# Triangular inverses of an RWKV-7 block: operands fetched two steps ahead, results written over them, a second buffer for the decays

## Chip, cores and metric

One core of one Trainium2 chip runs the whole kernel. The metric is device time in microseconds (us), the median of three runs.

## What is computed

Two layers of a block on 1280 tokens (256 of context, 1024 latent), 1024 wide. Each layer normalises, projects, mixes tokens in three ways (retention, gated linear attention, RWKV-7), projects back and runs a gated FFN. The part that matters here is RWKV-7's recurrence with six heads of 64, which the reference runs token by token, in both directions:

```python
def step(s, inp):
    rt, wt, kt, vt, kkt, at = inp
    sa = jnp.einsum("bhvk,bhk->bhv", s, -kkt)
    s = s * wt[:, :, None, :] + sa[..., None] * (kkt * at)[:, :, None, :] + vt[..., None] * kt[:, :, None, :]
    return s, jnp.einsum("bhvk,bhk->bhv", s, rt)
```

The kernel does it in chunks of 64 tokens. Within a chunk the rank-one corrections form a triangular system, so each chunk and head needs a 64x64 strictly triangular matrix (products of kk and kk*a, weighted by the decays between two tokens) and the inverse of one plus it.

## The kernel before

Operands lie with 128 channels on partitions (two heads a column block, three blocks). `rwkv_in` (L459) makes, by layer, the columns of RWKV's input projection; `col` (L487) is one column block: 72 or so dense products on TensorE, copied out by ScalarE, convolved by VectorE. Each finished row of operands (decay sums, kk, kk*a, k, r) goes to DRAM with `rw_row` (L648), in a tensor named `ops` that is indexed by 64-token chunk. Once decay sums, kk and kk*a are there, `rwkv_in` starts the generator `rw_inverses` (L681) and takes three or four of its steps between two columns of the rest of the projection (L600 to L606), and what is left at the end (L632). After that the next stage starts with the dense products of `gla_in` and the scan `rwkv` (L1233), which reads the inverses.

One step u of twenty (a forward and a backward chunk each) does this:

- X, a slot of tag `a` (AB = 5 slots), gets the chunk's operands from `ops` by two DMAs, one a direction (`rw_load`, L655 to L669, all issued by SyncE through L248). In traces this is `a<-ops`; the text calls the pair *fetch u*.
- ScalarE takes the exponential of the decay sums into P (one buffer, L671) and into X itself (L672), by L238.
- VectorE forms M in T, a second slot of tag `a`, by L679 and L694.
- TensorE multiplies (L701, through L245: `pn<-a`), VectorE masks the result into A, the last third of T (L702 through L640).
- A goes to DRAM (L703: `af<-a`); the text calls it *store u*.

After every fourth step `rw_inverse` (L708) reads four stored steps back (`L<-af`, four DMAs) and inverts their 32x32 diagonal blocks on GpSimd, some 60 instructions one after another (L718 to L728), then writes them out (`xe<-L`, `xe<-LT`, three DMAs each). There are five such recursions a layer.

The program is recorded in Python order, and a scheduler then orders each engine's instructions by priority and by when it expects operands and slots. Each engine, and SyncE's queue of DMAs, runs its list strictly in order. A DMA that has to wait for a semaphore therefore holds all DMAs behind it. Names in the queue beside the above: `wraw` weights, `gb` and `vt` finished results, `c<-ops` a row read back, `X<-ops`, `SAV`, `XE` the scan's operands.

```python
X = self.t(p, [128, PW], "a", bufs=AB)[:, 0:1152].rearrange(...)
ops = self.rw_load(l, P, X, u)
T = self.t(p, [128, PW], "a", bufs=AB)
```

Of the kernel before, what the change touches and what calls it, by code (L numbers as in the profile page):

```python
# [49 lines left out]
C2 = 1  # L50
PA = 7
NR = 2
AB = 5
HP = 5000,4500,4500
N1, N2 = 2,20
NS = 4
# [3 lines left out]
PW = TOK + 1  # L60
# [10 lines left out]
def rw_where(u):  # L71

    ns = [(0, 1), (1, 0)][u // 2] if u < 4 else (u // 2, 11 - u // 2)
    return [(ns[0], u % 2), (ns[1], 1 - u % 2)]
# [96 lines left out]
class Kern:  # L171
# [200 lines left out]

    def split_norm(self, x, b, A, B, s, xh, xl, pe=False):

        nc = self.nc
        n = BLK[b][1]
        rs = self.rstd(x, b, pe)
        for kt in range(KT):
            v = self.tmp()[:, :n]
            nc.vector.tensor_tensor(v, x[:, kt, :], rs, op=ALU.mult)  # L380
            self.act(v, v, AF.Identity, bias=B[:, kt, s:s + 1], scale=A[:, kt, s:s + 1])
            nc.scalar.copy(xh[:, kt, :], v)  # L382
            nc.vector.tensor_tensor(xl[:, kt, :], v, xh[:, kt, :].bitcast(F32), op=ALU.subtract)  # L383

    def norm_here(self, x, b, A, B, s):

        n = BLK[b][1]
        rs = self.rstd(x, b)
        for kt in range(KT):
            v = self.tmp()[:, :n]  # L390
            self.nc.vector.tensor_tensor(v, x[:, kt, :], rs, op=ALU.mult)
            self.act(x[:, kt, :], v, AF.Identity, bias=B[:, kt, s:s + 1], scale=A[:, kt, s:s + 1])

# [15 lines left out]
    def xn_tiles(self, blocks):  # L409
        xh, xl = {}, {}  # L410
        for b in blocks:
            A = self.A2 if b == 2 else self.A01
            xh[b] = self.t(A, [128, KT, BLK[b][1]], f"xh{b}", F32R)
            xl[b] = self.t(A, [128, KT, BLK[b][1]], f"xl{b}", F32R)
# [44 lines left out]
    def rwkv_in(self, l, V, W1, xh, xl, ctx_out):  # L459
# [56 lines left out]
        def zeros():  # L516
            if l:
                return
            zero = self.t(p, [128, PW], "a", bufs=AB)[:, 0:96]
            nc.gpsimd.memset(zero, 0.0)  # L520
# [44 lines left out]
        for j in range(3):  # L565
            a = self.t(p, [128, PW], "a", bufs=AB)
            for o, n in NB:
# [71 lines left out]
    def rw_masked(self, o, ps, m):  # L639
        self.nc.vector.tensor_tensor(o, ps, m.unsqueeze(1).to_broadcast([m.shape[0], 3, 64]), op=ALU.mult)  # L640

    def rw_P(self, p):
        P = self.t(p, [128, 2, 3, 66], "P")
        self.nc.gpsimd.memset(P[:, 0, :, 0:1], 1.0)
        self.nc.gpsimd.memset(P[:, 1, :, 65:66], 1.0)
        return P

# [4 lines left out]
            x = t[:, o:o + 64 * (c1 - c0)].rearrange("p (c x) -> p c x", x=64)  # L652
            self.dma(*((x, m) if back else (m, x)))

    def rw_load(self, l, P, X, u):  # L655


        half = float(np.exp(-0.5))
        lo = 15 - X.shape[2]
        src = self.OPS[l]  # L660
        r = []
        for d, (n, c) in enumerate(rw_where(u)):
            w = 2 * n + c
            if d == 0:
                self.dma(X[:, d], src[:, w, lo:15])
            else:
                if lo < 6:
                    self.dma(X[:, d, 0:6 - lo], src[:, w, lo:6])
                self.dma(X[:, d, 6 - lo:15 - lo], src[:, w, 9:18])  # L669
            cu, kk, kka = (X[:, d, o - lo:o - lo + 3] for o in ((12, 6, 9) if d else (6, 9, 12)))  # L670
            self.act(P[:, d, :, 1:65], cu, AF.Exp, scale=-half)  # L671
            self.act(cu, cu, AF.Exp, scale=half)  # L672
            r.append((cu, kk, kka))
        return r

    def rw_decayed(self, dst, ops, P):

        for d in range(2):
            self.nc.vector.tensor_tensor(dst[:, d, :, 0:64], ops[d][1], P[:, d, :, 2 * d:2 * d + 64], op=ALU.mult)  # L679

    def rw_inverses(self, l, p):  # L681

        nc = self.nc
        P = self.rw_P(p)
        for u in range(20):
            bi, w = u // 4, slice(6 * (u % 4), 6 * (u % 4) + 6)
            X = self.t(p, [128, PW], "a", bufs=AB)[:, 0:1152].rearrange("p (d i x) -> p d i x", d=2, x=64)
            ops = self.rw_load(l, P, X, u)
            T = self.t(p, [128, PW], "a", bufs=AB)
            M = T[:, 0:768].rearrange("p (d j x) -> p d j x", d=2, j=3)  # L690
            A = T[:, 768:1152].rearrange("p (h x) -> p h x", h=6)
            self.rw_decayed(M, ops, P)
            for d in range(2):
                nc.vector.tensor_tensor(M[:, d, :, 64:128], ops[d][2], ops[d][0], op=ALU.mult)  # L694
            for e in range(2):
                R = slice(64 * e, 64 * e + 64)
                ps = self.pn()
                for j in range(3):
                    for d in range(2):
                        a, k = M[R, d, j, 0:64], M[R, d, j, 64:128]  # L700
                        self.mm(ps[64 * d:64 * d + 64, 64 * j:64 * j + 64], *((a, k) if d else (k, a)))  # L701
                self.rw_masked(self.rw_heads(A, e), ps[:, 0:192].rearrange("p (j x) -> p j x", j=3), self.rwmask[:, 0:64])  # L702
            self.dma(self.AF[l][bi][:, w], A)  # L703
            if u % 4 == 3:
                self.rw_inverse(l, bi)
            yield
# [526 lines left out]
    def rwkv(self, l, V, ctx_out):  # L1233
# [7 lines left out]
        P = self.rw_P(p)  # L1241
# [5 lines left out]
        def pre(u):  # L1247
            out = ctx_out or u >= 4
            lo = 0 if out else 3
            X = self.t(p, [128, 2, 15, 64], "X", bufs=XB)[:, :, lo:15]  # L1250
            ops = self.rw_load(l, P, X, u)
            AR = self.t(p, [128, 2, 3, 128], "AR", bufs=NB)
            BK = self.t(p, [128, 2, 3, 128], "BK", bufs=2)
            PC = self.t(p, [128, 2, 3], "PC", bufs=NB)
# [63 lines left out]
        def step(u, B):  # L1318
            old = S[0]
            AR, SA, SR, BKT, SAV, PC, XE = (B[x] for x in ("AR", "SA", "SR", "BKT", "SAV", "PC", "XE"))  # L1320
            T = [slice(64 * d, 64 * d + 64) for d in D]
            O = [slice(64 - 64 * d, 128 - 64 * d) for d in D]
            pa = self.pr("a", 1)
            for h in range(6):
                for d in D:
                    self.mm(pa[T[d], 64 * h:64 * h + 64], SA[O[d], h, :], SAV[O[d], d, 64 * h:64 * h + 64],
                            start=h == 0, stop=old is None and h == 5)
            if old is not None:
                for j in range(3):
                    for d in D:  # L1330
                        self.mm(pa[T[d], 128 * j:128 * j + 128], AR[:, d, j, 0:64], old[:, d, j, :], start=False, stop=j == 2)
            R0 = self.t(p, [128, 384], "R0")
            nc.scalar.copy(R0, pa[:, 0:384])
            ps = self.pr("s", 1)
            for h in range(6):
                for d in D:
                    self.mm(ps[T[d], 64 * h:64 * h + 64], XE[T[d], h, 0:64], R0[T[d], 64 * h:64 * h + 64])
            nc.scalar.copy(SAV[T[0], 0, :], ps[T[0], 0:384])
# [41 lines left out]
        with hp(1):  # L1380
            cur = [pre(u) for u in range(2)]
        yield
        for u in range(20):
            with hp(0):
                step(u, cur[u])
            if u + 2 < 20:
                with hp(1):
                    cur.append(pre(u + 2))
            yield
# [587 lines left out]
```

## Time and profile before

| | |
|---|---|
| median of 3 runs | 4083.36 us (4080.87 to 4087.71) |
| profiled execution, its own time | 4084.64 us |
| its span, first to last instruction | 4082.9 us |
| TensorE busy | 3765.2 us, 92% |
| VectorE busy | 2572.8 us, 63% |
| ScalarE busy | 1779.2 us, 44% |
| GpSimd busy | 1570.2 us, 38% |
| DMA engines busy, own queue of SyncE | 47.1% |
| mean granted TensorE clock | 0.961 |

The span is a little shorter than the time, by what lies before the first and behind the last instruction. A busy TensorE is not one at its peak, since its instructions overlap; its idle time is what the views of waits explain. In rows of a timeline the column behind the start is the length; SyncE's rows show how long issuing took, not how long the transfer ran. "<-" after an idle time names what ended it.

### The profile page before, as it was taken

The numbers are of one execution on the slowest core, as the hardware profiler recorded it, in microseconds if no ns is written. First come the engines' busy times: TensorE is split into PE (matmuls) and PEld (weight loads), VectorE is DVE, ScalarE is ACT, GpSimd is POOL, SyncE is SP. The second block draws the span as 40 slices with busy tenths as digits, with TensorE's granted clock in tenths as the row PEclk, the third lists the DMA queues.
The fourth block names the chain that finished last, engine by engine and source line by source line (L and its number), as shares of the span: only waits on it lengthen the run. The fifth ranks groups of instructions, "written<-read, shape, count | busy, mean of one in ns | idle before, by whom it ended". The sixth has DMA issues, their size and how long they took to land. (4 is left out here: it accounts for less than half of the span.)

```text
span 4082.9 us, 78226 instructions
## 1 busy us (share of the span) xinstructions
PE 3765.2 (92%) x30344; PEld 3128.7 (77%) x30344; DVE 2572.8 (63%) x4522; ACT 1779.2 (44%) x3578; POOL 1570.2 (38%) x1714
## 2 busy tenths in 40 slices
PE   7998999889998999999979997999898988999998
PEld 4776888776687988888758676887766768999886
DVE  3565757667746766665862565667658578556666
ACT  5443334234436744443545443334234465434442
POOL 1155640333435823224436145740424443223443
PEclk9998999999999999999989998999989989999999
DMA  7487545566516522225424387555654232222542
GB/s 226 107 239 186 139 125 154 172 186 193 172 60 220 186 75 85 81 83 211 158 105 141 94 233 200 136 140 147 202 183 150 88 141 101 74 84 96 182 164 101
DMA packets 626355, 594.09 MB, mean 146 GB/s; under 512 B 315452, under 2 KB 517440, under 8 KB 607680
## 3 DMA queue, kind: packets, MB, share of 16 engines
q1 hardware_dynamic: 625696, 588.04, 47.1%
q8 instruction: 240, 3.93, 0.4%
q0 software_dynamic: 288, 1.05, 0.1%
q14 instruction: 131, 1.07, 0.1%
HBM read 442.67 MB, written 146.28 MB: 144 GB/s over the span
## 5 line engine op out<-in xcount | busy, mean ns | idle before, releaser
L1456 POOL TENSOR_TENSOR slo<-raw,shi 128x512 fp32r<-128x512 f32 x511 | 730.6, 1446 | 1082.1 <-ACT shi L1455 1004.8
L1455 ACT CAST shi<-raw 128x512 fp32r<-128x512 f32 x522 | 319.5, 621 | 520.3 <-PE pd L245 207.3
L439 POOL TENSOR_TENSOR wlo<-wraw,whi 128x512 fp32r<-128x512 f32 x120 | 168.8, 1415 | 413.1 <-ACT whi L438 407.3
L245 PE MATMUL pd<-wlo,xh 128*128 128x256 f32 x1072 | 315.1, 294 | 1.3 <-POOL wlo L439 1.3
L1746 DVE TENSOR_TENSOR f<-pm,f 128x512 f32<-128x512 f32 x320 | 219.5, 688 | 153.3 <-PE pm L245 152.1
L245 PE MATMUL pd<-whi,xh 128*128 128x256 f32 x1072 | 314.7, 295 | 0.5 <-DVE st L443 0.5
L245 PE MATMUL pd<-whi,xl 128*128 128x256 f32 x1072 | 313.7, 293 | 0.0
L245 PE MATMUL pm<-hh,shi 128*128 128x512 f32 x704 | 277.2, 395 | 9.8 <-ACT hh L1726 5.4
L245 PE MATMUL pd<-xh,whi 128*128 128x512 f32 (+1 forms) x720 | 273.2, 380 | 10.0 <-ACT xh L382 8.2
L245 PE MATMUL pm<-hl,shi 128*128 128x512 f32 x704 | 275.8, 392 | 0.3 <-DVE hl L1727 0.3
L245 PE MATMUL pm<-hh,slo 128*128 128x512 f32 x704 | 275.5, 391 | 0.0
L245 PE MATMUL pd<-xl,whi 128*128 128x512 f32 (+1 forms) x720 | 272.3, 379 | 3.3 <-DVE xl L383 3.1
L245 PE MATMUL pd<-xh,wlo 128*128 128x512 f32 (+1 forms) x720 | 270.8, 377 | 0.9 <-POOL wlo L439 0.8
L1455 ACT CAST shi<-tw 128x512 fp32r<-128x512 f32 x200 | 123.6, 620 | 305.7 <-PE pd L245 232.0
L245 PEld LDWEIGHTS pd<-wlo,xh 128*128 128x128 f32 x1072 | 211.0, 197 | 9.1 <-issue 5.4
L245 PEld LDWEIGHTS pd<-whi,xh 128*128 128x128 f32 x1072 | 210.4, 197 | 7.8 <-issue 3.1
L245 PEld LDWEIGHTS pd<-whi,xl 128*128 128x128 f32 x1072 | 210.7, 197 | 6.7 <-issue 4.7
L1456 DVE TENSOR_TENSOR slo<-tw,shi 128x512 fp32r<-128x512 f32 x200 | 143.7, 719 | 64.7 <-ACT shi L1455 64.4
L725 POOL TENSOR_TENSOR L<-L,itmp 96x30 f32<-96x30 f32 (+5 forms) x300 | 169.1, 564 | 21.9
L245 PEld LDWEIGHTS pd<-xh,whi 128*128 128x128 f32 x720 | 141.5, 197 | 43.2 <-ACT xh L382 11.8
L245 PEld LDWEIGHTS pd<-xl,whi 128*128 128x128 f32 x720 | 141.1, 196 | 36.8 <-issue 8.5
L723 POOL TENSOR_TENSOR itmp<-L 96x30 f32<-96x30 f32 (+5 forms) x300 | 159.4, 531 | 21.7 <-issue 0.2
(409 smaller groups left out, 11090.5 us busy)
## 6 DMA issues: line engine op xcount, KB each, us to landing
raw<-in_wgu SPq DMA_DIRECT2D x72, 1024.0 KB
raw<-in_wd SPq DMA_DIRECT2D x55, 1024.0 KB
wmod<-in_w_mod SPq DMA_DIRECT2D x192, 256.0 KB
wraw<-in_w_in SPq DMA_DIRECT2D x100, 256.0 KB
a<-ops SPq DMA_DIRECT2D x80, 288.0 KB
h<-h SPq DMA_DIRECT2D x44, 512.0 KB
h<-u SPq DMA_DIRECT2D x19, 1024.0 KB
X<-ops SPq DMA_DIRECT2D x36, 480.0 KB
```

What stands on the lines that cost most here:

```text
L245: return self.nc.tensor.matmul(out, l, r, start=start, stop=stop, skip_group_check=skip)
L439: nc.gpsimd.tensor_tensor(wl[i][:, :, w], r, wh[i][:, :, w].bitcast(F32), op=ALU.subtract)
L723: eng.tensor_tensor(t3, L3[:, 0:u, u:u + 1].to_broadcast([96, u, w]), L3[:, u:u + 1, u + 1:32].to_broadcast([96, u, w]), op=ALU.mult)
L725: eng.tensor_tensor(L3[:, 0:u, u + 1:32], L3[:, 0:u, u + 1:32], t3, op=ALU.subtract)
L1455: self.nc.scalar.copy(hi, src)
L1456: e.tensor_tensor(lo, src, hi.bitcast(F32), op=ALU.subtract)
L1746: nc.vector.tensor_tensor(facc[b][:, m, :], ps, facc[b][:, m, :], op=ALU.add)
```

## The change

The load is split into a fetch (`rw_fetch`, the DMAs) and the rest (`rw_load`). `rw_inverses` now issues, at the start of step u, the fetches up to step u+2 that aren't issued yet. The tag `a` has three slots instead of five, all for fetched operands: the result A is written over the first third of the fetched tile, and M gets a tag of its own, `ft`, with two buffers. P has a second buffer, in the pool `inv`, used by every other step. The scan `rwkv` calls fetch and load one behind the other, as before.

```diff
--- before.py
+++ after.py
@@ -50,7 +50,7 @@
 C2 = 1
 PA = 7
 NR = 2
-AB = 5
+AB = 3
 HP = 5000,4500,4500
 N1, N2 = 2,20
 NS = 4
@@ -639,8 +639,8 @@
     def rw_masked(self, o, ps, m):
         self.nc.vector.tensor_tensor(o, ps, m.unsqueeze(1).to_broadcast([m.shape[0], 3, 64]), op=ALU.mult)
 
-    def rw_P(self, p):
-        P = self.t(p, [128, 2, 3, 66], "P")
+    def rw_P(self, p, tag="P"):
+        P = self.t(p, [128, 2, 3, 66], tag)
         self.nc.gpsimd.memset(P[:, 0, :, 0:1], 1.0)
         self.nc.gpsimd.memset(P[:, 1, :, 65:66], 1.0)
         return P
@@ -652,13 +652,10 @@
             x = t[:, o:o + 64 * (c1 - c0)].rearrange("p (c x) -> p c x", x=64)
             self.dma(*((x, m) if back else (m, x)))
 
-    def rw_load(self, l, P, X, u):
-
-
-        half = float(np.exp(-0.5))
+    def rw_fetch(self, l, X, u):
+
         lo = 15 - X.shape[2]
         src = self.OPS[l]
-        r = []
         for d, (n, c) in enumerate(rw_where(u)):
             w = 2 * n + c
             if d == 0:
@@ -667,6 +664,13 @@
                 if lo < 6:
                     self.dma(X[:, d, 0:6 - lo], src[:, w, lo:6])
                 self.dma(X[:, d, 6 - lo:15 - lo], src[:, w, 9:18])
+
+    def rw_load(self, P, X):
+
+        half = float(np.exp(-0.5))
+        lo = 15 - X.shape[2]
+        r = []
+        for d in range(2):
             cu, kk, kka = (X[:, d, o - lo:o - lo + 3] for o in ((12, 6, 9) if d else (6, 9, 12)))
             self.act(P[:, d, :, 1:65], cu, AF.Exp, scale=-half)
             self.act(cu, cu, AF.Exp, scale=half)
@@ -681,14 +685,20 @@
     def rw_inverses(self, l, p):
 
         nc = self.nc
-        P = self.rw_P(p)
+        P2 = [self.rw_P(x, "P") for x in (p, self.inv)]
+        ahead = {}
         for u in range(20):
             bi, w = u // 4, slice(6 * (u % 4), 6 * (u % 4) + 6)
-            X = self.t(p, [128, PW], "a", bufs=AB)[:, 0:1152].rearrange("p (d i x) -> p d i x", d=2, x=64)
-            ops = self.rw_load(l, P, X, u)
-            T = self.t(p, [128, PW], "a", bufs=AB)
-            M = T[:, 0:768].rearrange("p (d j x) -> p d j x", d=2, j=3)
-            A = T[:, 768:1152].rearrange("p (h x) -> p h x", h=6)
+            for v in range(u, min(u + 3, 20)):
+                if v not in ahead:
+                    ahead[v] = self.t(p, [128, PW], "a", bufs=AB)
+                    self.rw_fetch(l, ahead[v][:, 0:1152].rearrange("p (d i x) -> p d i x", d=2, x=64), v)
+            X = ahead.pop(u)
+            P = P2[u % 2]
+            A = X[:, 0:384].rearrange("p (h x) -> p h x", h=6)
+            ops = self.rw_load(P, X[:, 0:1152].rearrange("p (d i x) -> p d i x", d=2, x=64))
+            T = self.t(p, [128, 768], "ft", bufs=2)
+            M = T.rearrange("p (d j x) -> p d j x", d=2, j=3)
             self.rw_decayed(M, ops, P)
             for d in range(2):
                 nc.vector.tensor_tensor(M[:, d, :, 64:128], ops[d][2], ops[d][0], op=ALU.mult)
@@ -1248,7 +1258,8 @@
             out = ctx_out or u >= 4
             lo = 0 if out else 3
             X = self.t(p, [128, 2, 15, 64], "X", bufs=XB)[:, :, lo:15]
-            ops = self.rw_load(l, P, X, u)
+            self.rw_fetch(l, X, u)
+            ops = self.rw_load(P, X)
             AR = self.t(p, [128, 2, 3, 128], "AR", bufs=NB)
             BK = self.t(p, [128, 2, 3, 128], "BK", bufs=2)
             PC = self.t(p, [128, 2, 3], "PC", bufs=NB)
```

No engine gets other arithmetic, but the scheduler orders the queues anew. Below are three places of SyncE's queue, first before, then after the change. A name's number tells tiles apart.

The head of layer 0's inverses, before: fetch 0 is tile 1352, fetch 1 is 1381, and store 0 is `af<-a_1359`.
```order
L248 DMA a_1352<-ops_12_81 128x576 x2
L248 DMA c_1853<-ops_12_81 128x16x64
L248 DMA wraw_2759<-in_w_in 128x4x128
L248 DMA wraw_2763<-in_w_in 128x4x128
L248 DMA vt_49_118<-vt_1860 128x2x128
L248 DMA a_1381<-ops_12_81 128x576 x2
L248 DMA af_32_101<-a_1359 128x384
L248 DMA vt_49_118<-vt_1868 128x4x128
```
After: fetches 0, 1 and 2 are tiles 1355, 1358 and 1361, and the last row is fetch 3.
```order
L248 DMA a_1355<-ops_12_81 128x576 x2
L248 DMA a_1358<-ops_12_81 128x576 x2
L248 DMA a_1361<-ops_12_81 128x576 x2
L248 DMA c_1862<-ops_12_81 128x16x64
L248 DMA wraw_2768<-in_w_in 128x4x128
L248 DMA wraw_2772<-in_w_in 128x4x128
L248 DMA vt_49_118<-vt_1869 128x2x128
L248 DMA af_32_101<-a_1355 128x384
L248 DMA a_1390<-ops_12_81 128x576 x2
```
Fetches 1 and 2 have moved ahead of the second part of `c<-ops`, two weight loads and `vt`; fetch 3 stands directly behind store 0.

The end of layer 0's inverses, before, from the write-back of the first recursion: fetch 17 is tile 2859, fetch 18 is 2888 (its two halves apart), fetch 19 is 2917; the stores are those of steps 14 to 16.
```order
L248 DMA xe_42_111<-L_1576 24x32x32 x3
L248 DMA vt_49_118<-vt_3143 128x2x128
L248 DMA a_2859<-ops_12_81 128x576 x2
L248 DMA af_35_104<-a_2567 128x384
L248 DMA xe_42_111<-LT_1672 24x32x32 x3
L248 DMA L_1933<-af_33_102 24x32x32 x4
L248 DMA a_2888<-ops_12_81 128x576
L248 DMA af_35_104<-a_2596 128x384
L248 DMA a_2888<-ops_12_81 128x576
L248 DMA vt_49_118<-vt_3151 128x4x128
L248 DMA af_36_105<-a_2729 128x384
L248 DMA a_2917<-ops_12_81 128x576 x2
```
After, from the same write-back: fetches 15, 16 and 17 are tiles 2403, 2569 and 2598; the stores are 13, 14 and 15.
```order
L248 DMA xe_42_111<-L_1585 24x32x32 x3
L248 DMA a_2403<-ops_12_81 128x576 x2
L248 DMA af_35_104<-a_2241 128x384
L248 DMA vt_49_118<-vt_3154 128x4x128
L248 DMA xe_42_111<-LT_1681 24x32x32 x3
L248 DMA L_1942<-af_33_102 24x32x32 x4
L248 DMA a_2569<-ops_12_81 128x576 x2
L248 DMA vt_49_118<-vt_3162 128x4x128
L248 DMA af_35_104<-a_2374 128x384
L248 DMA af_35_104<-a_2403 128x384
L248 DMA gb_14_83<-tt_3167 128x1281
L248 DMA a_2598<-ops_12_81 128x576 x2
```
Three fetches stood behind the write-back; now five do, since fetch 18 comes directly behind these rows, and fetch 19 behind `gb` and the stores of steps 16 and 17.

The end of layer 1's inverses, before: fetches 17, 18 and 19 are tiles 25231, 25260 and 25289, the stores are 16 to 19.
```order
L248 DMA xe_42_111<-LT_24094 24x32x32 x3
L248 DMA L_24355<-af_38_107 24x32x32 x4
L248 DMA a_25231<-ops_13_82 128x576 x2
L248 DMA gb_15_84<-tt_25536 128x1281
L248 DMA gb_15_84<-tt_25537 128x1281
L248 DMA af_41_110<-a_25126 128x384
L248 DMA a_25260<-ops_13_82 128x576 x2
L248 DMA af_41_110<-a_25238 128x384
L248 DMA a_25289<-ops_13_82 128x576 x2
L248 DMA af_41_110<-a_25267 128x384
L248 DMA af_41_110<-a_25296 128x384
```
After: fetches 15 to 19 are tiles 24803, 24969, 24998, 25131 and 25243; the stores are 14 to 18.
```order
L248 DMA xe_42_111<-LT_24106 24x32x32 x3
L248 DMA L_24367<-af_38_107 24x32x32 x4
L248 DMA a_24803<-ops_13_82 128x576 x2
L248 DMA a_24969<-ops_13_82 128x576 x2
L248 DMA af_40_109<-a_24774 128x384
L248 DMA a_24998<-ops_13_82 128x576 x2
L248 DMA af_40_109<-a_24803 128x384
L248 DMA af_41_110<-a_24969 128x384
L248 DMA a_25131<-ops_13_82 128x576 x2
L248 DMA a_25243<-ops_13_82 128x576 x2
L248 DMA af_41_110<-a_24998 128x384
L248 DMA af_41_110<-a_25131 128x384
```
Five fetches instead of three now stand behind the loads of the second recursion, in turn with the stores whose slots they take, and the two `gb` have moved ahead of those loads. On TensorE nine steps' products (11 to 19) now stand behind the last dense product of layer 1's projection, where eight (12 to 19) did; in layer 0 it is five (15 to 19) as before.

## Rows read from the trace of the kernel before

**Rows 1.** The page, part 1: busy us, share of span, instructions of each engine.
```profile
PE 3765.2 (92%) x30344; PEld 3128.7 (77%) x30344; DVE 2572.8 (63%) x4522; ACT 1779.2 (44%) x3578; POOL 1570.2 (38%) x1714
```

**Rows 2.** Busy us by stretch: length, engines (instructions), granted clock, DMA share, GB/s.
```profile
221.00:313.00 92.00, 86.53 (x706) 67.85 (x705) 62.54 (x112) 44.30 (x101) 54.41 (x81) 0.98 0.88 241
313.00:337.00 24.00, 13.65 (x138) 8.39 (x137) 10.82 (x30) 10.53 (x27) 8.61 (x21) 0.78 0.95 249
...
2450.00:2486.00 36.00, 17.90 (x195) 12.43 (x193) 19.51 (x45) 11.70 (x29) 17.07 (x36) 0.68 0.80 221
```

**Rows 3.** Waits of TensorE, 2380 to 2500 us: us in total, times, longest.
```profile
PE pn L245 <- DVE a L694: 18.9, 9, 5.7
```

**Rows 4.** By line, 313 to 337 us: busy, mean ns, idle before, releaser.
```profile
L679 DVE TENSOR_TENSOR a<-a,P 128x192 f32<-128x192 f32 x8 | 3.1, 386 | 11.5 <-ACT P L238 11.5
L238 ACT ACTIVATE P<-a 128x192 f32<-128x192 f32 x8 | 2.9, 363 | 11.7 <-DMA a<-ops 11.7
```

**Rows 5.** Timeline of GpSimd, layer 0: start, us, line, operation, idle before it.
```profile
262.35 0.16 POOL L718 MEMSET L<- 96x32 f32 x1 [7.24 <-DMA L<-af]
...
310.62 0.24 POOL L725 TENSOR_TENSOR L<-L,itmp 96x30 f32<-96x30 f32 x1
```

**Rows 6.** SyncE's queue, layer 0: start us, us issuing, line, transfer, count.
```profile
227.05 0.32 SPq L248 DMA_DIRECT2D af<-a  x1
...
231.81 1.32 SPq L248 DMA_DIRECT2D a<-ops  x2
...
251.25 4.16 SPq L248 DMA_DIRECT2D wraw<-in_w_in  x3
255.50 3.35 SPq L248 DMA_DIRECT2D L<-af  x4
...
310.88 4.08 SPq L248 DMA_DIRECT2D xe<-L  x3
...
317.23 3.53 SPq L248 DMA_DIRECT2D xe<-LT  x3
320.80 2.75 SPq L248 DMA_DIRECT2D L<-af  x4
...
326.12 0.58 SPq L248 DMA_DIRECT2D af<-a  x1
327.91 0.87 SPq L248 DMA_DIRECT2D a<-ops  x2
```

**Rows 7.** Waits of SyncE's queue, 215 to 337 us.
```profile
SPq L248 <- DMA af<-a: 1.9, 2, 1.1
```

**Rows 8.** Waits of SyncE's queue, 2380 to 2500 us.
```profile
SPq L248 <- DMA af<-a: 6.0, 3, 3.5
```

**Rows 9.** Tile a, layer 0: ns min/median/max, first and last start.
```profile
L679 DVE TENSOR_TENSOR a<-a,P x40: 345/422/3636, 222.0 to 334.1; 128x192 f32<-128x192 f32 x40
L694 DVE TENSOR_TENSOR a<-a x40: 341/358/784, 222.4 to 334.6; 128x192 f32<-128x192 f32 x40
L640 DVE TENSOR_TENSOR a<-pn,rwmask x40: 341/350/358, 226.2 to 336.6; 128x192 f32<-128x192 f32 x40
L248 SPq DMA_DIRECT2D af<-a x20: 319/389/1115, 227.1 to 337.0; - x20
```

**Rows 10.** Tile a, 2380 to 2520 us.
```profile
L248 SPq DMA_DIRECT2D af<-a x20: 319/320/2723, 2388.3 to 2494.8; - x20
```

**Rows 11.** Timeline of SyncE's queue, layer 1.
```profile
2464.96 1.80 SPq L248 DMA_DIRECT2D xe<-L  x3
...
2471.07 3.00 SPq L248 DMA_DIRECT2D xe<-LT  x3
2474.12 2.57 SPq L248 DMA_DIRECT2D L<-af  x4
...
2485.53 0.87 SPq L248 DMA_DIRECT2D a<-ops  x2
```

**Rows 12.** Timeline of TensorE, layer 1.
```profile
2460.76 0.74 PE L245 MATMUL pn<-a 64*64 64x64 f32 x24
```

## The prediction

> **What bounds the kernel now.** I read busy time first: TensorE is busy 92% of the span [rows 1], so only work that leaves TensorE idle is worth anything. The changed code runs in two short stretches, one for each layer, so I next read busy time by stretch. From 221 to 313 us, where the twenty inverse steps of layer 0 run beside the dense input projection, TensorE idles 5.5 us of 92. From 313 to 337 us, where the projection has run out and the last inverse steps are alone, it idles 10.35 of 24 (24.00 less 13.65). In layer 1 it idles 18.1 of 36 from 2450 to 2486 us [rows 2]. The reader should see in the same rows that the DMA engines are 0.80 to 0.95 busy there, and that the granted clock falls to 0.78 and 0.68. The waits then say what TensorE lacks: 18.9 us in nine waits on line 694, a product of a step's operands [rows 3]. One level further back, VectorE waits 11.5 us for ScalarE's exponential, and ScalarE 11.7 us for the fetch `a<-ops` [rows 4]. So the target is real: about 30 us of idle TensorE, 0.7% of the time, end in a late fetch. No other stretch is touched directly.
>
> Below, "fetch u" is the pair of DMAs that brings step u's operands, and "store u" is the `af<-a` that writes its result.
>
> **What the change does not add.** TensorE, VectorE and ScalarE run the same instructions, and SyncE issues the same number of DMAs. Four memsets on GpSimd for the second P cost nothing, since GpSimd then waits for data anyway: 7.24 us before its first recursion [rows 5]. The second P and the separate `ft` tile lift two waits between neighbouring steps; I cost them at nothing, because what ends last in the alone stretch is the fetch, not P [rows 4].
>
> **Is a fetch further ahead than before?** This decides the sign. Before, X and T of a step took two of five slots, so fetch u+3 needed a slot that step u or u+1 gives back. The trace shows where that put it: fetch 3 starts 4.8 us after store 0 (231.81 against 227.05), fetch 19 starts 1.8 us after store 16 (327.91 against 326.12); over the 17 such pairs of layer 0 the mean is 0.0 us [rows 6]. After, the result stands in the fetched tile, so with three slots fetch u+3 must wait until store u has landed. The depth of the pipeline is therefore the same three steps, and the order listing shows it: fetches 0 to 2 are bunched at the head, and behind that each fetch stands behind the store three steps earlier. What is new is that SyncE's queue, which runs in order, waits for a store's landing. The trace of before has five such waits: 1.9 us in two and 6.0 in three [rows 7, 8], 1.6 on average, from 0.95 to 3.5. I take 1.6. [...]
>
> **Layer 0's alone stretch.** Five steps (15 to 19) are uncovered before and after. Before, the queue reached the write-back of the first recursion at 310.88 us, the moment that GpSimd finished it [rows 5, 6]; call that G. Three fetches stood behind it, and store 19 came at 337.0 [rows 9], so at G+26.1. After, five stand behind it. Prices: `xe<-L` 4.1, `xe<-LT` 3.5, `L<-af` 2.75, a fetch 0.9, any other issue 0.4; from fetch to store 9.1 (327.91 to 337.0) and in layer 1 9.3 (2485.53 to 2494.8), so 9.2 [rows 6, 9, 10, 11]. Fetch 15 starts at G+4.1; one store, `vt`, `xe<-LT` and `L<-af` put fetch 16 at G+12.1; behind `vt`, stores 14 and 15, `gb` and a landing of 1.6, fetch 17 starts at G+15.0 and fetch 18 at G+15.9. Store 17 is 9.2 behind fetch 17, G+24.2; fetch 19 goes at G+24.6 and store 19 at G+33.8. At the same G that is **7.7 us later**. But G moves. The first recursion reads stores 0 to 3, and before its loads stood behind three weight loads that took 4.16 us (251.25 to 255.50) [rows 6]; now these come after it. GpSimd was free 7.24 us before its data came [rows 5], so G can come 0 to 7.2 us sooner. I take 4.2, the row that is moved: **+3.5 us**. Bounds: 7.7 and one longest landing instead of 1.6 (+1.9) make +9.6; 7.2 sooner, with the three small transfers at layer 1's prices (1.8, 3.0, 2.57, together 2.9 less) [rows 11], make -2.4.
>
> **Layer 1's alone stretch.** Before, eight steps were uncovered, the first product at 2460.76 [rows 12], the last store at 2494.8 [rows 10]. After, nine are: step 11 is pushed behind the last dense products. Its product starts 0.7 us sooner (one step of 0.74 less ahead of it), its store near 2462.0, its landing 2463.6. Then half of fetch 14, `xe<-L` (1.8), its other half, two stores, two `gb`, `xe<-LT` (3.0) and `L<-af` (2.57) put fetch 15 at 2473.5 and fetch 16 at 2474.4. Their stores are 9.2 behind, 2482.7 and 2483.6; fetch 19 waits for the landing of store 16, 2485.2, and store 19 comes at 2494.4: **-0.4 us**. Two landings lie on this chain: at 0.95 each it is -1.7, at 3.5 it is +3.4.
>
> **The sum.** +3.5 - 0.4 = +3.1 us on 4084.64, the profiled execution's own time, makes 4087.7. The median of the runs is 1.28 lower, so I forecast **4086.5 us**, which is no change: 0.2%, or 8.2 us, is about what a measurement of this kernel can tell from none. The forecast's own range adds both layers' bounds, -4.1 to +13.0: 4079.3 to 4096.4.
>
> **Rivals.**
> - *The fetches do come sooner (faster).* If every uncovered step finds its operands, it runs at VectorE's pace: two each of 0.422, 0.358 and 0.350 us [rows 9], 2.26 a step. Five steps take 11.3 instead of 24 us, nine take 20.3 instead of 34.0: -26.4, 4057 us; half of that is 4070. For it: the three fetches bunched at the head, and two P. Against it: five of layer 0's last fetches now stand behind `xe<-L`, three did before. The Trainium skill's page "Trainium Kernel Development and Optimization", section "Best Practices", asks to double-buffer so that DMA overlaps compute; by that rule alone this rival would hold in full.
> - *The ring of three paces the whole stage (slower).* Where before fetch u+3 went out together with store u (mean 0.0), it now follows by at least an issue of 0.3 and a landing of 1.6. Layer 0 has 17/3 = 5.7 turns of the ring: 10.8 us, if the stores and not TensorE's place in its own order set the pace. In layer 1 the mean distance was already over that, so I add nothing. 10.8 + 3.1 on 4083.36 is 4097.3. It decides from the point where fetch u+3, so delayed, lands after TensorE has reached step u+3. Against it: up to 313 us TensorE hides the steps.
> - *Weights come late (slower).* Fetches 1 and 2 are moved past one load of `c` and two of `wraw`: four issues of 0.43 and 1.18 MB at 241 GB/s [rows 2], 1.7 + 4.9 = 6.6 us a layer, 4096.6 in all. Against it: TensorE waits for no weight in these stretches; its cover is the projection already in hand. I give it little.
> - That the change does not do what its name says, fetch further ahead, is the forecast itself.
>
> **How the numbers follow.** Forecast 0.45, of which 0.05 lies over +8.2 us; faster rival 0.30; ring 0.20; weights 0.05. So faster 0.30, same 0.40, slower 0.05 + 0.20 + 0.05 = 0.30. The range reaches into the faster rival as far as 4066, which leaves out its better third (0.10), and to 4100, past the slower ones' 4097.3, which leaves out about 0.08.
>
> **What would show it.** In the changed kernel's trace: SyncE should wait for `af<-a` over twenty times where it did five; ScalarE's wait for `a<-ops` in the alone stretches should stay near 11 us; the loads `L<-af` of layer 0 should start near 247 to 251 us; store 19 should stand near 340 in layer 0 and 2494 (shifted by the first layer's change) in layer 1. I am wrong if TensorE's idle time in these stretches falls to a few us (the first rival), if the covered stretch before 313 us shows new waits on line 640 or 694 (the second), or on `wlo` (the third).

## The result, and the profile after

The changed kernel takes **4106.45 us** (median of 5 runs, 4099.35 to 4110.78), the kernel before 4083.36: 1.0054 times as long, 95% interval 1.0036 to 1.0071. It is slower by 23 us where 3 were forecast. The profiled execution's own time is 4106.45 us, its span 4104.7, 21.8 more than before. Of these, 5.7 us are longer busy time of TensorE and the other 16.1 idle time, by the page's first part (a second execution of the kernel before, e12 below, has a TensorE busy time 9.0 us longer than the first, so only the idle time says anything):

```profile
PE 3770.9 (92%) x30344; PEld 3129.8 (76%) x30344; DVE 2576.6 (63%) x4522; ACT 1774.7 (43%) x3578; POOL 1559.7 (38%) x1718
```

Busy time by stretch, the answer to [rows 2] (layer 1 is shifted by the 11 us that it starts later):

```profile
221.00:313.00 92.00, 87.77 (x709) 67.66 (x707) 58.00 (x108) 43.27 (x98) 52.24 (x81) 0.96 0.86 234
313.00:345.00 32.00, 12.91 (x135) 9.38 (x135) 15.58 (x34) 11.52 (x30) 19.25 (x39) 0.63 0.70 203
2461.00:2511.00 50.00, 21.84 (x267) 15.10 (x266) 26.87 (x59) 16.37 (x43) 28.59 (x60) 0.64 0.68 197
```

The covered stretch is as good as before: 4.2 us of TensorE idle instead of 5.5. The alone stretch of layer 0 lasts some 8 us longer and idles 19.1 us instead of 10.35; its granted clock is 0.63 instead of 0.78, so more of its products run at the lower level, 1.2 GHz. In layer 1, 28.2 of 50 us are idle, where the kernel before idles 22.7 in the same 50 us (2450 to 2500). TensorE's waits in 313 to 345 and in 2380 to 2515 us, beside [rows 3]:

```profile
PE pn L245 <- DVE ft L704: 14.2, 6, 4.7
...
PE pn L245 <- DVE ft L704: 22.8, 9, 9.8
```

One level back (by line, 313 to 345 us, as in [rows 4]) the late fetch is still there: ScalarE idles 20.4 us for it instead of 11.7, where the forecast expected about 11.

```profile
L683 DVE TENSOR_TENSOR ft<-a,P 128x192 f32<-128x192 f32 x10 | 5.8, 579 | 11.9 <-ACT P L238 11.9
...
L238 ACT ACTIVATE P<-a 128x192 f32<-128x192 f32 x10 | 3.6, 362 | 20.6 <-DMA a<-ops 20.4
```

Why the fetch is late stands in SyncE's queue. These are its waits, first of the kernel before, then of the change; in each, layer 0 (215 to 345 us) ahead of the "..." and layer 1 (2365 to 2520 us) behind it. Columns: us in total, times, longest. The landings before are in [rows 7, 8].

```profile
SPq L248 <- DVE a L640: 11.9, 5, 3.5
SPq L248 <- DVE a L694: 7.8, 7, 2.9
...
SPq L248 <- DVE a L640: 25.7, 12, 6.2
SPq L248 <- DVE a L694: 9.9, 5, 3.2
```

```profile
SPq L248 <- DVE a L640: 27.0, 12, 6.6
SPq L248 <- DMA af<-a: 15.0, 7, 3.4
...
SPq L248 <- DVE a L640: 18.9, 11, 6.0
SPq L248 <- DMA af<-a: 15.4, 6, 4.8
```

Such a row adds up waits of stores, for their results, and of fetches, for a slot. So the trace has to be read by the transfer that each wait holds back. Before, eight of the twelve waits for L694 (VectorE's last read of an operand tile) were stores'. Fetches waited for VectorE 17.4 us in 8 waits (four of them for L694) and for a landing 7.9 us in 5. With the change, no fetch waits for VectorE, and all 30.4 us in 13 waits for landings are fetches'.

Plainer is the distance from store u to fetch u+3, by their starts in SyncE's timeline. Its mean over the 17 pairs was 0.0 us in layer 0 and 2.2 in layer 1, and 8 and 4 of the fetches went ahead of the store, as fetch 17 did here, ahead of store 14 (timeline of SyncE, before):

```profile
315.74 0.91 SPq L248 DMA_DIRECT2D a<-ops  x2
316.75 0.38 SPq L248 DMA_DIRECT2D af<-a  x1
```

With the change the means are 4.6 and 4.8 us, and no fetch goes ahead of its store. In layer 0 all seven landing waits fall before 304 us. In the alone stretch behind that, no fetch waits for its slot: the five that are left stand in the queue behind the write-back and behind stores that wait for their results.

### The profile page after: what moved, and what is told of

Read it like the earlier page. It is cut to its first block, busy times and chain, and to the rows that moved or that the text cites. A ratio compares the mean times of both kernels' runs of the same rounds, so it can differ in the third digit from the quotient of the medians.

```text
span 4104.7 us, 78196 instructions
## 1 busy us (share of the span) xinstructions
PE 3770.9 (92%) x30344; PEld 3129.8 (76%) x30344; DVE 2576.6 (63%) x4522; ACT 1774.7 (43%) x3578; POOL 1559.7 (38%) x1718
## 5 line engine op out<-in xcount | busy, mean ns | idle before, releaser
L735 POOL TENSOR_TENSOR L<-L,itmp 96x30 f32<-96x30 f32 (+5 forms) x300 | 166.2, 554 | 21.9
L245 PEld LDWEIGHTS pd<-xh,whi 128*128 128x128 f32 x720 | 141.7, 197 | 42.3 <-ACT xh L382 13.2
L245 PEld LDWEIGHTS pd<-xh,wlo 128*128 128x128 f32 x720 | 141.3, 196 | 32.4 <-issue 7.5
```

The lines of the kernel that those rows point to most:

```text
L245: return self.nc.tensor.matmul(out, l, r, start=start, stop=stop, skip_group_check=skip)
L735: eng.tensor_tensor(L3[:, 0:u, u + 1:32], L3[:, 0:u, u + 1:32], t3, op=ALU.subtract)
```

## Where the 22 us arise

TensorE runs the same matmuls in every kernel here. So each matmul can be found in two traces, by the names of its tiles and its rank among those, and the difference of its two starts is TensorE's delay at that place. The table gives the median delay over 12 us around a time of the first trace of before. 337 to 345 us is the end of layer 0's inverses, 2350 lies before layer 1's, 2515 behind them.

| run | ratio to before | SyncE's waits for landings, layers 0 / 1 | store u to fetch u+3, us | delay at 345 | 820 | 1250 | 1450 | 2350 | 2515 | 4060 us |
|---|---|---|---|---|---|---|---|---|---|---|
| the change | 1.0054 | 15.0 / 15.4 us | 4.6 / 4.8 | 7.8 | 2.0 | 4.6 | 11.1 | 11.2 | 15.2 | 22.6 |
| the change again (e8) | 1.0064 | 13.6 / 13.9 | 4.3 / 4.8 | 5.3 | -2.0 | 1.1 | 8.4 | 7.1 | 9.4 | 15.9 |
| before again (e12) | | 2.4 / 4.8 | 0.2 / 2.3 | -1.9 | 1.0 | 6.2 | 6.3 | 2.8 | 2.5 | 9.5 |
| e1, one P | 1.0056 | 14.7 / 14.0 | 4.5 / 4.7 | 9.0 | -0.9 | 4.8 | 10.0 | 9.1 | 12.0 | 27.4 |
| e3, half `ft`, 3 slots | 1.0044 | 21.9 / 14.9 | 4.7 / 4.8 | 8.8 | 1.5 | 0.0 | 3.5 | 0.3 | 2.9 | 7.8 |
| e5, one step ahead | 1.0049 | 17.1 / 9.3 | 4.1 / 4.4 | 8.0 | -10.4 | -1.8 | 7.9 | 8.1 | 9.7 | 23.0 |
| e6, stores from ScalarE | 1.0042 | 31.2 / 32.0 | 4.8 / 4.9 | 6.1 | -7.7 | -4.6 | 0.6 | -2.7 | 0.9 | 4.0 |
| e4, 4 slots | 0.9988 | 6.2 / 3.1 | -0.5 / -0.9 | -4.4 | -6.4 | -2.6 | 1.6 | 1.8 | 0.7 | 2.9 |
| e10, own tile x3, K in place | 1.0002 | 0.6 / 0.7 | -1.6 / -1.0 | -1.4 | -11.3 | -1.6 | -0.4 | -1.0 | -7.2 | 4.3 |
| e2, own tile | 0.9965 | none | -9.2 / -8.7 | -10.6 | -11.3 | 5.7 | 5.9 | 5.9 | -12.0 | -0.5 |
| e2 again (e11) | 0.9979 | none | -9.2 / -8.7 | -10.9 | -8.9 | 3.9 | 2.7 | 3.0 | -15.6 | -13.6 |
| e7, own tile, one ahead | 0.9990 | none | -9.3 / -8.7 | -12.3 | -19.2 | -3.5 | -2.1 | -1.1 | -19.2 | -17.9 |
| e9, own tile, none ahead | 0.9981 | none | -9.5 / -8.6 | -9.6 | -10.3 | 3.9 | 3.8 | 3.8 | -13.6 | -2.5 |

The ratios are of several runs, the delays of one execution. Two executions of the kernel before lie up to 9.5 us apart in this table, so only differences that repeat are read. (The traces of e3 and e6 are of their fastest executions, 4091.53 us where the median is 4107.27, and 4087.87 where it is 4092.37; their delays say less than their ratios.) Four repeat: the inverse stages (column 345, and 2350 to 2515), a gain of 5.8 and 7.3 us between 345 and 820 in the two traces of the change (before again loses 2.9 there), a step of 6 to 7 us between 1250 and 1450 in the same two, and a loss of 13 to 17 us between 820 and 1250 in the four executions with a tile of its own in two buffers (e2, e11, e7, e9). What the change loses behind 2515, 7.4 and 6.5 us, before again loses too (7.0).

Two things follow. What a run wins or loses in layer 0 does not last: at 1250 us all rows lie between -4.6 and 6.2, in no order of column 345. And the distance from store u to fetch u+3 splits the runs as their ratios do: with 4.1 to 4.9 us the ratios are 1.0042 to 1.0064, with a distance below zero 0.9965 to 1.0002, and no interval of one group reaches into the other (lowest 1.0024, highest 1.0017).

## The experiments

The runs come from three chips: e1 to e4, e5 to e8, e9 to e12. Ratios are against the kernel before on the same chip (medians 4086.2, 4079.5 and 4085.0 us), so times of different groups cannot be compared as they stand.

**e1, the second buffer alone taken back.**

```diff
-        P2 = [self.rw_P(x, "P") for x in (p, self.inv)]
+        P = self.rw_P(p)
...
-            P = P2[u % 2]
```

> The change with a single buffer for the decays again. Theory 1, the ring (a fetch waits for the landing of the store three steps back, since the result lies in the fetched tile): the second P buys nothing, so the first X<-ops, which stands right behind the last store, stays near 345 us in layer 0 and near 2511 in layer 1 (before: 337.4 and 2495.5), and the time near 4106 us. Theory 2, the order of SyncE's queue (fetches that stand behind xe<-L, xe<-LT, L<-af and the stores' own waits for VectorE): the same. Theory 3, the reordering of later stages (7 to 8 of the 22 us arise outside the two inverse stages, where no edit was made): with the inverse stages unchanged, the rest of the program can still move by several us either way, 4100 to 4112 us.

1.0056 (1.0038 to 1.0073); the first `X<-ops` at 345.20 and 2507.50 us. The second P is worth nothing that can be measured, as costed.

**e2, the result in a tile of its own** (with one P, to make room).

```diff
-            A = X[:, 0:384].rearrange("p (h x) -> p h x", h=6)
+            A = self.t(p, [128, 384], "fa", bufs=2).rearrange("p (h x) -> p h x", h=6)
```

> As e1, but the result is written to a small tile of its own (two buffers), not over the operands, so that a fetch's slot is free as soon as VectorE and ScalarE have read it. Theory 1: SyncE's waits for the landing of af<-a in the two stages (15.0 us in 7 and 15.4 us in 6 with the change) fall to under 5 us each, the first X<-ops comes back to 336 to 340 us in layer 0 and some 5 us sooner in layer 1, and the time falls by about 14 us to some 4092 (4084 to 4098). Theory 2: the fetches still stand behind the recursion's transfers and the stores, X<-ops stays within 2 us of 345 and 2511, time 4100 to 4112. Theory 3 adds up to 6 us either way to both.

0.9965 (0.9945 to 0.9984), 4076.49 us: faster than the kernel before, and faster than the 4084 to 4098 expected. SyncE's waits of e2 in layer 0 have no row for a landing any more. Of the 16 waits below, eight are fetches', for VectorE; the others are mostly stores':

```profile
SPq L248 <- DVE fa L640: 11.7, 12, 1.9
...
SPq L248 <- DVE ft L703: 4.6, 4, 2.3
```

Timeline of SyncE and busy time of e2: the scan's first fetch comes 18.6 us sooner than with the change (344.83) and 11.2 sooner than before (337.42), ten sooner than expected, and the stretch that idled 19.1 us idles 6.4.

```profile
326.27 2.15 SPq L248 DMA_DIRECT2D X<-ops  x3
```

```profile
313.00:345.00 32.00, 25.62 (x255) 20.72 (x254) 14.27 (x32) 11.31 (x34) 20.17 (x41) 0.89 0.97 254
```

**e3 and e4, three slots and four.** Both write K over one of its own operands, so that `ft` is half as large; e4 uses the room for a slot.

```diff
-            T = self.t(p, [128, 768], "ft", bufs=2)
+            T = self.t(p, [128, 384], "ft", bufs=2)
...
-                nc.vector.tensor_tensor(M[:, d, :, 64:128], ops[d][2], ops[d][0], op=ALU.mult)
+                nc.vector.tensor_tensor(ops[d][2], ops[d][2], ops[d][0], op=ALU.mult)
...
-                        a, k = M[R, d, j, 0:64], M[R, d, j, 64:128]
+                        a, k = M[R, d, j], ops[d][2][R, j]
```

```diff
-AB = 3
+AB = 4
```

> The change, with the second factor K written over one of its own operands in the fetched tile, so that the separate tile is half as large; three slots as in the change. It is the control for e4. Theories 1 and 2: a slot is freed no sooner and no later than in the change (its store's landing ends it), X<-ops near 345 and 2511, time near 4106. Theory 3: 4100 to 4112.

> As e3, with a fourth slot in the room that e3 freed. Theory 1: a fetch now waits for the store four steps back, which has landed by then; SyncE's waits for the landing of af<-a fall to under 5 us in each stage, X<-ops comes at 336 to 340 us in layer 0 and some 5 us sooner in layer 1, time 4084 to 4098. Theory 2: nothing moves, X<-ops within 2 us of 345 and 2511, time 4100 to 4112. Theory 3 adds up to 6 us either way.

e3: 1.0044 (1.0026 to 1.0061), `X<-ops` at 345.03. e4: 0.9988 (0.9971 to 1.0005), `X<-ops` at 333.85, a little sooner than expected. The two kernels differ in the slot alone, and one slot undoes the loss: 22 us between their medians. SyncE's waits of e4, layer 0 and layer 1:

```profile
SPq L248 <- DMA af<-a: 6.2, 7, 1.9
...
SPq L248 <- DMA af<-a: 3.1, 3, 1.7
```

**e5, one step ahead instead of two.**

```diff
-            for v in range(u, min(u + 3, 20)):
+            for v in range(u, min(u + 2, 20)):
```

> The change with fetches recorded one step ahead instead of two; three slots and the result over the operands as in the change. Ring theory (the slots, freed by a store's landing, set when a fetch may go): the recorded distance does not matter, the first X<-ops stays within 3 us of 345 in layer 0, the time is 4100 to 4114. If the distance in the program does help, as the change means it to, this loses it: X<-ops 5 us or more later in each layer and a time of 4115 or more.

1.0049 (1.0029 to 1.0070), `X<-ops` at 345.07: with three slots that a landing frees, the distance in the program changes nothing.

**e6, the stores from another queue.**

```diff
-            self.dma(self.AF[l][bi][:, w], A)
+            self.nc.scalar.dma_start(out=self.AF[l][bi][:, w], in_=A)
```

> The change with the stores af<-a issued from ScalarE's queue instead of SyncE's, so that no fetch stands in order behind a store that still waits for VectorE (27.0 us in 12 such waits of SyncE in layer 0 with the change). Ring theory: a fetch still waits for the landing of the store three steps back, X<-ops stays at 342 to 348 us in layer 0, time 4100 to 4112. In-order theory: the fetches go when their slots are free and nothing is lost behind stores, X<-ops at 334 to 340, time 4080 to 4095.

1.0042 (1.0024 to 1.0059). `X<-ops` came at 336.05 and the median is 4092.37, both of which the in-order theory expected. But on this chip the kernel before takes 4079.52, so the ratio is the ring theory's; and the landmark was badly chosen, as store 19 no longer stands ahead of it in that queue. The last inverse product shows the stage itself: 340.93 us, with the change 342.60 and 340.68 (e8), before 335.22. The 27.0 us for L640 fell to 0.8, and waits for landings took their place, 25.2 and 26.0 us of them of fetches (waits of SyncE in both layers, then TensorE's last group of products in layer 0):

```profile
SPq L248 <- DMA af<-a: 31.2, 14, 6.1
...
SPq L248 <- DMA af<-a: 32.0, 10, 7.4
```

```profile
340.93 1.17 PE L245 MATMUL pn<-ft 64*64 64x64 f32 x20 [0.70 <-DVE ft L704]
```

So the place in the queue is not what costs: freed from it, a fetch follows its store by 4.8 us as before, and waits for its slot.

**e7 and e9, the distance with early slots.** To e2's edit, in e7 and in e9:

```diff
-            for v in range(u, min(u + 3, 20)):
+            for v in range(u, min(u + 2, 20)):
```

```diff
-            for v in range(u, min(u + 3, 20)):
+            for v in range(u, min(u + 1, 20)):
```

> As e2 (result in a tile of its own), with fetches recorded one step ahead instead of two. If what e2 won is the early release of the slots alone, this is as fast as e2: first X<-ops within 3 us of e2's 326.5 us in layer 0, time 4068 to 4085. If it also needs the distance of two steps, X<-ops comes 5 us or more later than in e2 and the time is 4085 to 4095.

> As e2 (result in a tile of its own, three slots for operands alone), with each fetch recorded in its own step, as in the kernel before: the release of the slots without the fetch ahead. If the early release is all that counts, since the scheduler moves a fetch up as far as its slot allows, the first X<-ops comes within 3 us of e2's 326.5 us in layer 0 and the time is 0.995 to 1.001 of before. If the recorded distance counts, X<-ops comes 5 us or more later than in e2 and the time is 1.000 to 1.005 of before.

e7: 0.9990 (0.9968 to 1.0012), `X<-ops` at 325.05. e9: 0.9981 (0.9965 to 0.9998), at 327.31. The scheduler moves a fetch up as far as its slot allows; two steps, one or none in the program are the same within the intervals.

**e8 and e12, second executions of the change and of before**, without an edit.

> The changed kernel once more, for a second profiled execution. If the 8 us outside the two inverse stages come from the new order of the instructions, the second trace shows the same delay against before within 3 us at each landmark (layer 1's start some 11 us late, the end some 22). If they are the chance of one execution (where the granted clock falls), the stages show the same 7 and 4 to 7 us, and the rest differs by 5 us or more from the first trace. Time 4099 to 4112.

> The kernel before once more, for a second profiled execution against which the others are read: its landmarks agree with the first trace within 3 us at the end of both inverse stages. If the first trace of before was a lucky one outside these stages, this one is later by 5 us or more at the end of the span; if not, within 5 us.

e8: 1.0064 (1.0043 to 1.0085). Its delays behind layer 0's inverses are 2.5 to 4.1 us below the first trace's up to 2350 us and 6.7 below at the end; e12 ends 9.5 us behind the first trace of before. Both expectations were met in part: the inverse stages, the gain behind 345 and the step behind 1250 us repeat, the rest is mostly chance. By e12's test the first trace of before was a lucky one behind its inverse stages; by the times it is typical (4084.64 us) and e12's single run a long one (4094.42, where the median on its chip is 4084.98).

**e10, a version meant to beat all.** To e3's edit:

```diff
-            A = X[:, 0:384].rearrange("p (h x) -> p h x", h=6)
+            A = self.t(p, [128, 384], "fa", bufs=3).rearrange("p (h x) -> p h x", h=6)
```

> A version meant to beat both: result in a tile of its own with three buffers, K over one of its operands as in e3 (so a slot is free when TensorE has read it, a little later than in e2), two buffers for the decays. Ring theory: no wait of a fetch for a landing, first X<-ops at 326 to 332 us in layer 0, time 0.993 to 1.000 of before. If the gain of e2 hung on the slot being free before the products, X<-ops comes at 332 or later and the time is over 1.000.

1.0002 (0.9987 to 1.0017), `X<-ops` at 335.40. It hardly waits for landings (0.6 and 0.7 us), yet stays 9 us behind e2 at `X<-ops`. That is what was expected if e2's gain hung on the slot's being free before the products: a slot is now free only when TensorE has read K in it. It is the likeliest reason, but the parts of this version were not tried one by one.

**e11, e2 again**, without an edit.

> The kernel of e2 once more, with a second profiled execution. Time 0.994 to 0.999 of before. In e2's trace 29 us were won in the two inverse stages and most were lost again between 820 and 1250 us (17 us) and behind 3000 us (10 us). If the order of the later instructions loses them, the second trace loses over 10 us between 820 and 1250 us again; if it was the chance of that execution, it loses under 6.

0.9979 (0.9964 to 0.9993), 4076.16 us. e2 is the fastest version found, 0.2 to 0.35% below the kernel before; the intervals of e7 and e9 overlap with its own.

## What e2 gives back

e2 wins 28.5 us in the two inverse stages (10.6, and 17.9 between 2350 and 2515), e11 29.5, but their ratios stand for 14 and 9 us of 4085. Most goes between 820 and 1250 us, in both traces (e2 loses another 11.5 behind 2515, e11 only 2.0). Busy time there, the same matmuls in each (before, e2, e11; the stretches shifted by the table's delays):

```profile
820.00:1250.00 430.00, 390.56 (x3164) 295.99 (x3164) 281.86 (x636) 179.87 (x433) 159.10 (x155) 0.96 0.51 162
```

```profile
808.70:1255.70 447.00, 403.79 (x3162) 306.33 (x3163) 289.44 (x644) 177.03 (x435) 159.57 (x156) 0.93 0.50 157
```

```profile
811.10:1253.90 442.80, 399.34 (x3163) 303.85 (x3163) 286.24 (x643) 176.82 (x435) 162.33 (x156) 0.94 0.50 159
```

Of e2's 17.0 us more, 13.2 are the same matmuls run longer, at a mean granted clock of 0.93 instead of 0.96; idle time grows by 3.8. What brings the clock down there, the new order of the instructions or the earlier arrival, was not tried apart and stays open. The earlier arrival has this for it: e5 and e10, without e2's tile and 10.4 and 11.3 us early at 820, lose 8.6 and 9.7 there as well, while no run that comes less than 8 us early loses over 5.7.

## Why the prediction was wrong

Two steps failed: one of the mechanism, the depth of the ring, and one term put at nothing, the stretches that are not edited.

- **The depth of the ring.** "The depth of the pipeline is therefore the same three steps" does not follow from the mean of 0.0 us beside it. That mean says that before, about half of layer 0's fetches u+3 went ahead of store u, and so did not wait for it: of five slots one could also be an operand's, free as soon as VectorE had read it. With the change every slot holds a result and is free only when that has landed, and the mean is 4.6 us (4.8 instead of 2.2 in layer 1). e4 (one more slot) and e2 (own tile) take the whole loss away; e1, e5 and e6 do not. That the loss hangs on the slots is shown by this; where along the span it arises is shown only in part, below.
- **The landing wait**, taken as 1.6 us, measured 2.1 (15.0 in 7) and 2.6 (15.4 in 6), up to 4.8 where 3.5 was the longest seen. The forecast's 0.95 was the mean of two, not the shortest, which was 0.8. The number of these waits was 13, not over twenty.
- **Layer 0, +3.5 forecast, +7.4 measured** (+5.5 in e8; both inside -2.4 to +9.6). The five fetches behind the write-back were there; 1.7 us are G, 2.2 the way from G to store 19. The gate: `L<-af` went at 250.18, as forecast, and the first recursion started 3.3 us sooner (259.08 against 262.35 in [rows 5]), but G came at 308.36, 2.5 us sooner and not 4.2. Behind it, by the timeline of SyncE, fetch 16 (320.00) is at G+11.6 where G+12.1 was forecast; fetches 17 and 18 at G+17.8 instead of G+15.0, fetch 19 at G+28.3 instead of G+24.6. Store 17, the second of the pair at 329.29, holds fetch 19 behind it. The landing that the forecast put before fetch 17 was over by then. The last row is tile `a`'s: store 19 at 344.4, G+36.0 for G+33.8.

```profile
308.36 1.88 SPq L248 DMA_DIRECT2D xe<-L  x3
...
320.00 1.17 SPq L248 DMA_DIRECT2D a<-ops  x2
321.27 0.37 SPq L248 DMA_DIRECT2D vt<-vt  x1
321.74 3.73 SPq L248 DMA_DIRECT2D af<-a  x2
325.75 0.32 SPq L248 DMA_DIRECT2D gb<-tt  x1
326.16 2.48 SPq L248 DMA_DIRECT2D a<-ops  x4
...
329.29 7.25 SPq L248 DMA_DIRECT2D af<-a  x2
336.63 0.88 SPq L248 DMA_DIRECT2D a<-ops  x2
```

```profile
L248 SPq DMA_DIRECT2D af<-a x20: 319/331/2702, 226.3 to 344.4; - x20
...
L248 SPq DMA_DIRECT2D af<-a x20: 319/326/3187, 2399.6 to 2510.8; - x20
```

- **Layer 1, -0.4 forecast, +4.8 measured** (2510.8 less the 11.2 us of late start, against 2494.8), outside -1.7 to +3.4; e8 has +3.1, just inside. By SyncE's timeline `xe<-L` took 2.62 us and `xe<-LT` 5.09 where 1.8 and 3.0 were taken [rows 11], which is 2.9; with the longer landings the last two fetches went from 2499.43 on, where the last was forecast for 2496.4 (2485.2 and 11.2).

```profile
2474.67 2.62 SPq L248 DMA_DIRECT2D xe<-L  x3
...
2479.98 5.09 SPq L248 DMA_DIRECT2D xe<-LT  x3
...
2499.43 2.31 SPq L248 DMA_DIRECT2D a<-ops  x4
```

- **No other stretch was priced**, since "no other stretch is touched directly", and the delays of the two stages were added as if they lasted. The stages together are +12.2 us (+8.6 in e8), inside the forecast's own -4.1 to +13.0; what carries the time past the range lies outside them. Layer 0's delay is caught up by 820 us (see the table), for a reason that no run isolates. The scheduler gave later stages another order, too. Between 1250 and 1450 us the change loses 6.5 and 7.3 us (second trace) where before again loses 0.1. TensorE's waits from 1345 to 1455 us in before and the change, and VectorE's queue in each:

```profile
PE pd L245 <- DVE u L1611: 1.7, 1, 1.7
```

```profile
PE pd L245 <- DVE u L1622: 5.8, 3, 2.7
```

```profile
1356.62 0.69 DVE L391 TENSOR_TENSOR pm<-f,pn 128x512 f32<-128x512 f32 x1
1357.22 0.74 DVE L1611 TENSOR_TENSOR u<-pd,g 128x256 f32<-128x256 f32 x2
1357.89 0.68 DVE L391 TENSOR_TENSOR pm<-f,pn 128x512 f32<-128x512 f32 x1
```

```profile
1355.60 1.87 DVE L391 TENSOR_TENSOR pm<-f,pn 128x512 f32<-128x512 f32 x3
...
1360.81 1.36 DVE L391 TENSOR_TENSOR pm<-f,pn 128x512 f32<-128x512 f32 x2 [1.01 <-ACT f L238]
...
1369.13 0.74 DVE L1622 TENSOR_TENSOR u<-pd,g 128x256 f32<-128x256 f32 x2
```

  Before, the pair `u<-pd,g` that TensorE waits for stands among the `pm<-f,pn`; with the change it stands behind them and starts twelve us later. The wait is 6.2 us in the change's second trace and 1.7 in e2 and e11, which kept the old order; 4 of the 6.5 us are shown by it. It was seen in traces, not undone by an edit, and it is not the whole of it: e3 kept the old order there (1.8 us) and is 1.0044 all the same.
- **The rivals.** The slower one named the right mechanism, a ring of three with a landing in it, but put its price where TensorE covers it (221 to 313 us idles no more than before) and none in layer 1, where the distance was thought to be long enough and rose from 2.2 to 4.8 us. Its 4097.3 and the range's 4100 fell short. The faster one's -26.4 us is what e2 wins in the inverse stages (28.5) once the result leaves the slot. The Trainium skill's rule cited there ("Trainium Kernel Development and Optimization", section "Best Practices": double-buffer, so that DMA overlaps compute) held only then: a fetch ahead came sooner once VectorE's read, and no longer a landing, freed its slot. Weights were not late: TensorE's waits for `wlo` in the inverse stages are 0.6 us.
- **Right:** the second P at nothing (e1), the sooner `L<-af`, the fetch as what TensorE lacks in the alone stretches, and that the fetches do not come sooner.

## What to carry to other kernels

Count a ring's depth from the event that frees a slot: a result written over its operands turns "free when read" into "free when landed", and needs a slot more for it. Read a queue's waits by the transfer that each one holds back, and the distance between a store and the fetch that takes its slot: a mean near zero means that many fetches do not wait for that store. A delay in one stage may be caught up in the next, so it cannot simply be added to the total. Where a scheduler orders the whole program, a local edit moves stages a thousand us later, so look for gains and losses along the span before judging the edit by the total.

## What was not expected of the hardware

VectorE's product of two tiles in SBUF was mostly slower where GpSimd was busy. Timeline of VectorE with the change: the same L704 takes 0.36 us at 315 and 0.76 at 332, while L640, whose first operand is in PSUM, stays at 0.34. In the stretches below (columns as in [rows 2], the fifth engine is GpSimd) GpSimd is idle in the first and busy 4.45 of 5 us in the second. The six L704 between 326 and 336 us, with GpSimd at work throughout, took 0.36 (the first) and 0.56 to 0.76.

```profile
315.02 0.36 DVE L704 TENSOR_TENSOR ft<-a 128x192 f32<-128x192 f32 x1
...
332.36 0.76 DVE L704 TENSOR_TENSOR ft<-a 128x192 f32<-128x192 f32 x1
...
335.06 0.34 DVE L640 TENSOR_TENSOR a<-pn,rwmask 128x192 f32<-128x192 f32 x1
```

```profile
314.00:317.00 3.00, 0.01 (x1) 0.01 (x1) 2.06 (x7) 2.10 (x6) 0.00 (x0) 1.00 1.05 268
331.00:336.00 5.00, 2.18 (x28) 1.65 (x28) 4.96 (x10) 2.27 (x7) 4.45 (x8) 0.50 0.67 241
```

The Trainium skill's "VectorE: DVE Perf Modes", section "Two Vector instructions with no wait between them", says that VectorE's second read interface to SBUF is shared with GpSimd; these rows agree, and no run separates it from other causes. The prediction's 2.26 us a step took medians, among them 0.358 for this product, near the undisturbed price.

TensorE's clock can be low while it is busy: in e2 it was busy 3.03 of 6 us, and then ran 13 us at 0.50, the lower level, of which it was busy 12.18.

```profile
900.00:906.00 6.00, 3.03 (x22) 1.59 (x20) 5.93 (x10) 3.91 (x11) 5.77 (x6) 0.98 0.96 325
906.00:919.00 13.00, 12.18 (x74) 8.57 (x73) 6.65 (x14) 0.69 (x2) 3.31 (x4) 0.50 0.57 196
```
